# A build-time scheduler of a decoder trunk: transfers on one modelled rate, a reload in four lanes, a merge by accumulating transfers

## The chip, the cores and the metric

The kernel runs on one core of one Trainium2 chip. The metric is the device time of one execution in microseconds (us); the time before is the median of three runs. Engines are named as in the profile: PE (TensorE matmul), PEld (TensorE weight load), DVE (VectorE), ACT (ScalarE), POOL (GpSimd) and SP (SyncE, which here only issues transfers).

## The reference

One layer of a hybrid decoder trunk for a sequence of 512 tokens and 1024 channels in float32. Three token mixers stand side by side; their outputs go through one matrix each, are gated per channel, added, projected and added to the input.

```python
h = rmsnorm(x, norm_g)
proj = jnp.einsum('bsd,dn->bsn', h, w_in)
(aq, ak, av, ao, az, ai, af, bq, bk, bv, bz, bf, cu, cz, gates) = jnp.split(proj, SPLIT_POINTS, axis=-1)
...
yA = (hA.reshape(B, S, ML_WIDTH).astype(x.dtype) * ml_norm_g
      * jax.nn.sigmoid(ao) * jax.nn.silu(az))
...
yB = hB.reshape(B, S, FOX_WIDTH) * jax.nn.silu(bz)
...
ys = jnp.stack([yA, yB, yC], axis=2)
yb = jnp.einsum('bsnw,nwd->bsnd', ys, w_branch)
g = jax.nn.sigmoid(gates.reshape(B, S, N_BRANCH, D_MODEL))
merged = jnp.sum(g * yb, axis=2)
return x + jnp.einsum('bsd,de->bse', merged, w_out)
```

hA comes from a chunked mLSTM with 4 heads, hB from a forgetting attention with 8 heads, yC from a causal pooling with 4 groups. A last rmsnorm follows.

## The kernel before, in words

**Arithmetic.** Every float32 operand is split into a rounded part hi (a cast on ACT, line L291) and a remainder lo (a subtraction on DVE, L294); a product is three matmuls, hi·hi, hi·lo and lo·hi (`mm3`, L303 to L305). Activations stand channel by token: a weight tile of 128x128 is held in PE while 512 tokens (or 256) stream past.

**Weights.** They come from DRAM either as a unit (`feed_unit`: one transfer of 512 KB, L343 on SP, into a tile `raw`, then hi on ACT and lo on DVE) or as a pair (`feed_pair`). A pair serves two output chunks by seven products of half size in place of eight (a Strassen scheme). For it two transfers on SP (L379 of 512 KB, L383 of 768 KB) fill a tile `R`, and a third on POOL adds 512 KB to a part of it while it lands (L386, accumulating); two sums on DVE follow (L297). Out of R come four parts, numbered 0 to 3 in the trace of the order (hi_0, lo_0, ... hi_3, lo_3): part 1 comes straight from the L383 transfer, parts 2 and 3 need the sums. `raw` and `R` share three buffers. A pair's product writes three banks, named x, yz and y4 (the last prints as y); ACT copies a bank out (`side`, L497, L499; for the turned pairs of V L566) before PE may write the next product into it.

**Order of the work.** The four mixers' projections, heads and gates run first; then the three branches through their matrices, n = 0, 2, 1 in that order (wb in the trace), the merge, the output projection (out) and the last norm. The middle branch (n = 2, the pooling one) uses pairs whose moving operands ycs2, ycs3, ycs4 are sums made in `sides_c` (L1668 on); the last branch (n = 1, the attention) reads units. Branch outputs were written to DRAM (y) as they were made; `reload` (L1617) brings them back: eight transfers of 256 KB (`yf`, L1628) with a cast to hi and a lo each. Gates come back the same way (`gt`, L1752, 256 KB each).

**The scheduler.** Nothing is reordered on the chip: each engine runs its queue in the order in which the program emitted it, and a queue's head that waits holds all behind it. The order is fixed while the kernel is built, by the class `Flow`. Work beside the matmuls is written as chains, generators that yield (engine, cost, earliest start); `Flow` keeps a model clock for every engine, and emits the chain step that could start first, with a priority number to break ties. What a transfer takes is a constant in such a chain: a 512 KB raw unit lands 4.2 us after its issue whatever else is in flight, an R half 4.5 or 5.0, the accumulating part 6.2, a yf tile 6.0, and an issue on SP costs 0.06 us. So an instruction that waits for a transfer is put into its engine's queue where the model thinks that the transfer has landed.

**The merge of the middle branch** (L1789 to L1803): for each of four pairs, DVE multiplies two 128x512 halves of the result `ybc` by their gates (L1797), and then adds the whole 128x1024 tile to `mg` (the list `merged`), the running sum of the branches:

```python
                t = yield ("DVE", v_cost(D), t)
                add(merged[i], merged[i], c_)
                fl.put("C", 1, t)
```

The last branch adds to the same tiles: `gt<-wb,gt` (L1772), then `mg<-mg,gt` (L297), then the split into m for the output projection.

Of the kernel before, what the change touches and what calls it, by code (L numbers as in the profile page):

```python
# [10 lines left out]
ALU = mybir.AluOpType  # L11
# [3 lines left out]
S = 512  # L15
# [17 lines left out]
RAWS = 3  # L33

# [67 lines left out]
def a_cost(n):  # L102
    return 0.2 + 0.83e-3 * n
# [12 lines left out]
class Flow:  # L116
# [6 lines left out]
    def __init__(self):  # L123
        self.t = {"PE": 0.0, "DVE": 0.0, "ACT": 0.0, "POOL": 0.0, "SP": 0.0}
        self.func = None
        self.chains = []
        self.free = {}
        self.done = {}
        self.pos = 0

# [122 lines left out]
def trunk(tc, x, xt_in, w, wpair, cols, fg, out):  # L253
    nc = tc.nc
    with contextlib.ExitStack() as ctx:
# [75 lines left out]
        def feed_unit(i):  # L331
            what = order[i][1:]
            n = width(what)
            own = what[0] == "pw"
            prio = late(i, 0)

            def gen():
                if not own:
                    ts = yield ("get", "slot", 1)
                t = yield ("get", "R", 1)  # L340
                t = yield ("SP", 0.06, t)
                raw = raw_tile(f"raw{i}", n)
                nc.sync.dma_start(out=raw, in_=w[index[i]][:, :n])  # L343
                if own:
                    yield ("wait", ("av", AH - 1))
                    ts = yield ("get", "v", 1)
                t = max(t + 4.2, ts)
# [12 lines left out]
            fl.add(gen(), prio)  # L360

        def feed_pair(i, ps=None, q=None):
# [11 lines left out]
            def load():  # L374
                t = yield ("get", "R", 1)
                t = yield ("SP", 0.06, t)
                r = raw_tile(f"R{i}_{q}", 5 * Q)
                cell.append(r)
                nc.sync.dma_start(out=r[:, 3 * Q:].rearrange("p (a c) -> p a c", a=2),  # L379
                                  in_=src.rearrange("p (a c) -> p a c", c=Q)[:, 0:3:2])  # L380
                t1 = t + 4.5
                t = yield ("SP", 0.06, t)
# [538 lines left out]
        def emat(h):  # L921
# [4 lines left out]
            t = yield ("SP", 0.06, max(t, tw))  # L926
            nmb = work(f"nmb{h}")
            nc.sync.dma_start(out=nmb, in_=rows[h:h + 1, :].partition_broadcast(P))
            t = yield ("POOL", 0.9, t + 6.8)
# [105 lines left out]
        def values_a(h):  # L1035
# [68 lines left out]
            t = yield ("SP", 0.06, t)  # L1104
            nc.sync.dma_start(out=yd[0, h], in_=env["g"])
            fl.put("C", 1, t + 4.5)
            fl.done["y", 0, h] = t + 6.0
# [228 lines left out]
        def store(dst, tl, key, t):  # L1336
            def gen():
                t_ = yield ("SP", 0.06, t)
                nc.sync.dma_start(out=dst, in_=tl)
                fl.put("C", 1, t_ + 4.5)  # L1340
                fl.done[key] = t_ + 6.0
            fl.add(gen(), 0)
# [132 lines left out]
        def fox_pair(hp):  # L1475
            zB = [None]

            def head(h, cell, t_in):
# [14 lines left out]
                tn = yield ("SP", 0.2, tn)  # L1493
# [5 lines left out]
                tn += 8.0  # L1499
# [117 lines left out]
        def reload(n, homes, prio):  # L1617
# [4 lines left out]
            def one(i, c):  # L1622
# [19 lines left out]
            for i in range(4):  # L1642
                for c in range(2):
                    fl.add(one(i, c), prio)
# [32 lines left out]
        def sides_c():  # L1677
# [5 lines left out]
            for q in (2, 3, 0, 1):  # L1683
                for i in range(2):
                    ty = yield ("wait", ("y", 2, 2 * (q % 2) + i))
                    t = yield ("SP", 0.06, max(t, ty))
                    nc.sync.dma_start(out=f_[q][:, 2 * i:2 * i + 2],
                                      in_=yd[2, 2 * (q % 2) + i][:, :, (q // 2) * H:(q // 2 + 1) * H])
                tq.append(t + 9.0)
# [19 lines left out]
            t = max(tq)  # L1709
            yield from parts("A22", 3, home(0), t)  # L1710
# [35 lines left out]
        def load_gate(n, d):  # L1746
            def gen():
                tw = yield ("get", "w", 1)
                tg = yield ("wait", ("g", n, d // 2))
                t = yield ("SP", 0.06, max(tw, tg))  # L1750
                g_ = gate[n, d] = work(f"gt{n}{d}")
                nc.sync.dma_start(out=g_, in_=gd[n, d // 2][:, d % 2])  # L1752
                fl.done["gt", n, d] = t + 4.6
# [225 lines left out]
```

## Time and profile before

| | us |
|---|---|
| median of 3 runs | 856.97 (854.39, 856.97, 857.01) |
| profiled execution, whole time | 853.38 |
| its span | 851.4 |
| PE busy in the span | 835.8 (98%) |
| DVE busy | 663.1 (78%) |
| ACT busy | 535.4 (63%) |
| POOL busy | 114.0 (13%) |
| DMA, mean rate over the span | 187 GB/s, 158.96 MB |

The span is what the profiler saw of one execution; 2.0 us lie around it. A share is a share of the span. PE is one long stream of matmuls, so the rows to look for are those in which PE has a hole: in a timeline the idle time before an instruction stands in brackets, with the instruction whose end let it go.

### The profile page before, as it was taken

Reading aid. Unit: us, or ns where it says so; the run is one execution under the profiler, and the core shown is the slowest. Engines: PE = TensorE matmul, PEld = TensorE weight load, DVE = VectorE, ACT = ScalarE, POOL = GpSimd, SP = SyncE. Lnnn points to the kernel's source line nnn. Section 1 sums busy time; section 2 is a strip of 40 time slices with the busy share of each in tenths; the row PEclk is TensorE's granted clock in tenths of the full one; section 3 lists DMA queues with packets and bytes.
Section 4 is the critical chain, followed back from the end, with each engine's and each line's share of the span. In section 5 each row is a group of like instructions: output and inputs, shape, how many; then the busy total and the mean of one; then the engine's idle time right before and its main releaser. Section 6 shows DMA issues by size and latency. Waiting matters only on the chain.

```text
span 851.4 us, 15247 instructions
## 1 busy us (share of the span) xinstructions
PE 835.8 (98%) x6026; PEld 792.1 (93%) x6026; DVE 663.1 (78%) x1042; ACT 535.4 (63%) x906; POOL 114.0 (13%) x145
## 2 busy tenths in 40 slices
PE   9999999999999999999899999999999999999997
PEld 7888899999999999999899999999999988998886
DVE  5788998687998777988589788888887576986623
ACT  7569778757967857555367667568587553633223
POOL 0001422111111011010212111221220001010020
PEclk9999999999999999999999999999999999999999
DMA  9327866675774658487548878388865689576202
GB/s 342 110 75 221 215 172 173 194 203 117 214 191 112 186 159 215 136 251 195 153 161 219 225 179 241 91 208 246 239 143 199 206 280 321 157 275 219 102 22 99
DMA packets 62854, 158.96 MB, mean 187 GB/s; under 512 B 5428, under 2 KB 10932, under 8 KB 62784
## 3 DMA queue, kind: packets, MB, share of 16 engines
q1 hardware_dynamic: 47136, 126.96, 42.0%
q0 software_dynamic: 14928, 29.91, 20.9%
q10 hardware_dynamic: 720, 1.13, 0.4%
q8 instruction: 47, 0.77, 0.4%
q14 instruction: 23, 0.19, 0.1%
HBM read 143.27 MB, written 14.70 MB: 186 GB/s over the span
## 4 chain that ended last, share of the span: by engine, by line
PE 45%; DVE 2%; issue 1%; DMA 1%; ACT 1%; SPq 0%; DVEq 0%; ACTq 0%
PE wb L304 2%; PE wb L303 2%; PE wb L305 2%; PE out L304 2%; PE out L305 2%; PE out L303 2%; PE tpB L1562 1%; DMA yf<-y 1%; DVE lo L294 1%; DVE ycf L1703 1%; PE sB L304 0%; PE sB L303 0%; PE oB L303 0%; PE oB L304 0%; PE oB L305 0%
## 5 line engine op out<-in xcount | busy, mean ns | idle before, releaser
L294 DVE TENSOR_TENSOR lo<-R_None,hi 128x1024 fp32r<-128x1024 f32 (+1 forms) x184 | 197.8, 1091 | 30.2 <-ACT hi L291 29.7
L291 ACT CAST hi<-R_None 128x1024 fp32r<-128x1024 f32 (+1 forms) x184 | 169.1, 945 | 45.4 <-DVE R_None L297 26.0
L386 POOL DMA_DIRECT2D R_None<-w_pairs x46 | 56.0, 1217 | 461.4 <-DMA R_None<-w_pairs 211.5
L294 DVE TENSOR_TENSOR lo<-raw,hi 128x1024 fp32r<-128x1024 f32 (+3 forms) x45 | 51.5, 1151 | 25.7 <-ACT hi L291 25.4
L291 ACT CAST hi<-raw 128x1024 fp32r<-128x1024 f32 (+3 forms) x45 | 44.2, 994 | 40.9 <-DMA raw<-w_units 34.6
L297 DVE TENSOR_TENSOR R_None<-R_None 128x512 f32<-128x512 f32 x92 | 63.3, 689 | 2.5 <-DMA R_None<-w_pairs 1.7
L294 DVE TENSOR_TENSOR lo<-R,hi 128x1024 fp32r<-128x1024 f32 (+1 forms) x24 | 25.9, 1095 | 14.9 <-ACT hi L291 14.7
L291 ACT CAST hi<-R 128x1024 fp32r<-128x1024 f32 (+1 forms) x24 | 22.0, 942 | 8.7 <-DVE R L297 7.2
L304 PE MATMUL out<-lo,m 128*128 128x512 f32 (+1 forms) x72 | 26.3, 366 | 0.0
L303 PE MATMUL out<-hi,m 128*128 128x512 f32 (+1 forms) x72 | 26.3, 366 | 0.0
L305 PE MATMUL out<-hi,m 128*128 128x512 f32 (+1 forms) x72 | 26.3, 365 | 0.0
L1502 POOL TENSOR_SCALAR_AFFINE_SELECT nfb<-nfb 128x128 f32<-128x128 f32 x32 | 19.1, 731 | 31.1 <-DMA nfb<-rows 30.8
L1830 DVE TENSOR_TENSOR res<-out,res 128x512 f32<-128x512 f32 (+1 forms) x9 | 5.7, 632 | 18.4 <-PE out L305 18.2
L1833 ACT ACTIVATE fsq<-res 128x512 f32<-128x512 f32 (+1 forms) x9 | 5.3, 585 | 23.1 <-DVE res L1830 23.1
L291 ACT CAST m<-mg 128x512 fp32r<-128x512 f32 x8 | 5.0, 620 | 23.5 <-DVE mg L297 23.4
L1539 ACT ACTIVATE s<-s,mn 128x128 f32<-128x128 f32 (+3 forms) x32 | 17.8, 556 | 1.4 <-DVE mn L1528 1.3
L1528 DVE CUSTOM_DVE_ANT_0 s<-sB,nfb 128x128 f32<-128x128 f32 (+3 forms) x32 | 14.4, 485 | 4.0 <-issue 3.9
L303 PEld LDWEIGHTS out<-hi,m 128*128 128x128 f32 x72 | 13.6, 189 | 2.3
L304 PEld LDWEIGHTS out<-lo,m 128*128 128x128 f32 x72 | 13.6, 189 | 2.2
L305 PEld LDWEIGHTS out<-hi,m 128*128 128x128 f32 x72 | 13.6, 189 | 2.2
L386 POOL DMA_DIRECT2D R<-w_pairs x6 | 7.2, 1206 | 51.8 <-DMA R<-w_pairs 18.8
L1857 POOL TENSOR_TENSOR res<-res,fgb 128x512 f32<-128x512 f32 x4 | 5.2, 1296 | 65.3 <-ACT fsq L1833 65.1
(2495 smaller groups left out, 3533.2 us busy)
## 6 DMA issues: line engine op xcount, KB each, us to landing
R_None<-w_pairs SPq DMA_DIRECT2D x46, 768.0 KB, 6.9
R_None<-w_pairs SPq DMA_DIRECT2D x46, 512.0 KB, 4.8
R_None<-w_pairs POOLq DMA_DIRECT2D x46, 512.0 KB, 6.9
raw<-w_units SPq DMA_DIRECT2D x38, 512.0 KB, 4.5
g<-g SPq DMA_DIRECT2D x12, 512.0 KB, 5.4
gt<-g SPq DMA_DIRECT2D x24, 256.0 KB, 5.4
R<-w_pairs SPq DMA_DIRECT2D x6, 768.0 KB, 5.8
yf<-y SPq DMA_DIRECT2D x16, 256.0 KB, 6.3
```

Of the source, the lines that this page charges most:

```text
L291: nc.scalar.copy(out=hi, in_=full)
L294: nc.vector.tensor_tensor(out=lo, in0=full, in1=hi.bitcast(F32), op=ALU.subtract)
L297: nc.vector.tensor_tensor(out=out_, in0=a, in1=c, op=ALU.add)
L303: nc.tensor.matmul(out_, lhsT=ah, rhs=bh, start=start, stop=False, **kw)
L304: nc.tensor.matmul(out_, lhsT=ah, rhs=bl, start=False, stop=False, **kw)
L305: nc.tensor.matmul(out_, lhsT=al, rhs=bh, start=False, stop=stop, **kw)
L386: nc.gpsimd.dma_start(out=r[:, 3 * Q:].rearrange("p (a c) -> p a c", a=2), in_=src[:, 3 * Q:].unsqueeze(1).to_broadcast([P, 2, Q]), accum_ ...
L1502: nc.gpsimd.affine_select(out=nf[i][:, i * P:], in_=nf[i][:, i * P:], pattern=[[-1, P]], compare_op=ALU.is_ge, fill=NEG, base=0, channel_m ...
L1528: nc.vector.tensor_tensor_reduce(out=ss[i][:, :n], in0=os_[i][:, :n], in1=nf[i], scale=-P ** -0.5, scalar=-NEG, op0=ALU.add, op1=ALU.min, ...
L1539: nc.scalar.activation(out=s_, in_=s_, func=AF.Exp, bias=ms[i][0], scale=-1.0, accum_out=sme)
L1562: nc.tensor.transpose(tp[:, i * P:(i + 1) * P], ss[i][:, q0:q0 + P], ident)
L1703: nc.vector.tensor_tensor(out=f_[o], in0=f_[a_], in1=f_[c_], op=op)
```

## The change

It has four parts; what is computed stays the same, and so do all matmuls.

1. All modelled transfers share one rate. A new method `land` keeps the time at which the modelled bus comes free: a transfer lands 2.2 us after its issue or when the bus is free, whichever is later, plus its size over 260 KB per us (180 for accumulating ones, 100 and 150 for rows spread over the partitions). Every fixed landing is replaced by it, and an issue on SP costs 0.35 to 0.73 us in the model in place of 0.06 (2.9 for the four transfers of `nfb`), an accumulating issue on POOL 1.2 in place of 0.9.
2. The last branch is reloaded in four lanes of two tiles each, one after the other, at priority 1; before, eight chains stood side by side at priority 2.
3. The middle branch is merged by transfers: an accumulating transfer of 512 KB on POOL's queue from `ybc` to `mg` in place of the add on DVE, four times.
4. `sides_c` starts its A22 part when the second of four loads has landed in the model, not when all have.

```diff
+LATENCY = 2.2
...
+    def land(self, t, kb, rate=260.0):
+
+        self.bus = max(t + LATENCY, self.bus) + kb / rate
+        return self.bus
...
-                t = yield ("SP", 0.06, t)
+                t = yield ("SP", 0.55, t)
                 r = raw_tile(f"R{i}_{q}", 5 * Q)
...
-                t1 = t + 4.5
-                t = yield ("SP", 0.06, t)
+                t1 = fl.land(t, 512)
+                t = yield ("SP", 0.6, t)
                 nc.sync.dma_start(out=r[:, :3 * Q], in_=src[:, :3 * Q])
-                fl.done["R", me] = t + 5.0
-                t = yield ("POOL", 0.9, t1)
+                fl.done["R", me] = fl.land(t, 768)
+                t = yield ("POOL", 1.2, t1)
...
-                fl.done["T", me] = t + 6.2
+                fl.done["T", me] = fl.land(t, 512, 180.0)
...
-                tn = yield ("SP", 0.2, tn)
+                tn = yield ("SP", 2.9, tn)
...
-                tn += 8.0
+                tn = fl.land(tn - 2.0, 640, 150.0)
...
-        def reload(n, homes, prio):
+        def reload(n, homes, prio, lanes=8):
...
-                t = yield ("SP", 0.06, max(tw, ty))
+                t = yield ("SP", 0.73, max(tw, ty))
                 f_ = work(f"yf{n}{i}{c}")
                 nc.sync.dma_start(out=f_, in_=yd[n, i][:, c])
+                landed = fl.land(t, 256)
                 th = yield ("wait", ("home", n, i))
-                t = yield ("ACT", a_cost(S), max(t + 6.0, th))
+                t = yield ("ACT", a_cost(S), max(landed, th))
...
-            for i in range(4):
-                for c in range(2):
-                    fl.add(one(i, c), prio)
+
+            def lane(j):
+                for k in range(j, 8, lanes):
+                    yield from one(k // 2, k % 2)
+            for j in range(lanes):
+                fl.add(lane(j), prio)
...
-            t = max(tq)
-            yield from parts("A22", 3, home(0), t)
+            yield from parts("A22", 3, home(0), tq[1])
...
-        reload(1, home("yb"), 2)
+        reload(1, home("yb"), 1, 4)
...
-                t = yield ("DVE", v_cost(D), t)
-                add(merged[i], merged[i], c_)
-                fl.put("C", 1, t)
+                t = yield ("POOL", 1.2, t)
+                nc.gpsimd.dma_start(out=merged[i], in_=c_, accum_op=ALU.add)
+                fl.put("C", 1, fl.land(t, 512, 180.0))
```

Since the model decides the order, the numbers move instructions all over the program. Three places follow. In the rows an instruction stands with its line, its operation and its tiles; the number after a tile's name is a buffer's. Lines of the changed kernel lie 7 to 15 further down: L298 is the cast to hi, L301 lo, L304 the sum, L505 and L507 the copies of a bank, L574 that of a turned pair, L387, L391 and L394 the transfers of a pair, L1508 those of nfb, L1639 yf, L1767 gt, L1816 the new accumulating transfer.

**ACT, at the pair of bv in the attention heads** (`vbv_bv_1`, a turned pair whose weights stand in R_0 and R_1; hi_1 from R_None is a part of the next pair's weights). Before:

```order
L291 CAST dh_4607<-pb_4854 128x512
L291 CAST hi_1_5021<-R_None 128x512
L291 CAST hi_2_5024<-R_0_4656 128x1024
L566 COPY vbv_bv_1e_5041<-vbv_bv_1x 128x512
L291 CAST hi_2_5072<-R_1_4817 128x1024
L291 CAST hi_3_5082<-R_0_4656 128x1024
L291 CAST qkh_5105<-bqk_4989 128x1024
```

With the change:

```order
L298 CAST dh_4611<-pb_4837 128x512
L298 CAST hi_2_5042<-R_0_4667 128x1024
L298 CAST hi_2_5048<-R_1_4819 128x1024
L574 COPY vbv_bv_1e_5058<-vbv_bv_1x 128x512
L298 CAST hi_1_5089<-R_None 128x512
L298 CAST qkh_5085<-bqk_4991 128x1024
L298 CAST hi_3_5112<-R_0_4667 128x1024
L298 CAST hi_3_5134<-R_1_4819 128x1024
```

The cast hi_1 has moved behind both hi_2 and the copy of bank x; both hi_3 still stand behind it.

**ACT, at the first pair of the middle branch** (`wb_0_wb_1`; the four copies free its banks; yb0h, yb1h are casts of the last branch's reloaded tiles yf). Before:

```order
L497 COPY wb_0_wb_1e<-wb_0_wb_1x 128x256
L291 CAST yb0h<-yf_8732 128x512
L291 CAST hi_2_8794<-R_None 128x1024
L291 CAST yb0h<-yf_8734 128x512
L497 COPY wb_0_wb_1e<-wb_0_wb_1yz 128x256
L291 CAST yb1h<-yf_8736 128x512
L291 CAST yb1h<-yf_8738 128x512
L499 ACTIVATE wb_0_wb_1e<-wb_0_wb_1x 128x256
L291 CAST hi_3_8835<-R_None 128x1024
L497 COPY wb_0_wb_1e<-wb_0_wb_1y_8821 128x256
```

With the change:

```order
L505 COPY wb_0_wb_1e<-wb_0_wb_1x 128x256
L505 COPY wb_0_wb_1e<-wb_0_wb_1yz 128x256
L507 ACTIVATE wb_0_wb_1e<-wb_0_wb_1x 128x256
L505 COPY wb_0_wb_1e<-wb_0_wb_1y_8799 128x256
L298 CAST hi_2_8826<-R_None 128x1024
L298 CAST hi_1_8844<-R_None 128x512
L298 CAST hi_3_8848<-R_None 128x1024
L298 CAST hi_0_8871<-R_None 128x1024
L298 CAST yb0h<-yf_8743 128x512
```

No cast of a reloaded tile stands between the four copies any more; the first comes behind the four parts of the next pair.

**POOL, from the last attention head to the end of the middle branch.** Before:

```order
L1502 AFFINE_SELECT nfb_7485<-nfb_7485 128x128 x4
L1488 COPY qkf_7596<-bqk_7566 128x256
L386 DMA R_None<-w_pairs 128x2x512
L1502 AFFINE_SELECT nfb_7685<-nfb_7685 128x128 x4
L386 DMA R_None<-w_pairs 128x2x512 x5
L1813 DMA fgb<-final_g_in 128x1024
```

With the change:

```order
L1513 AFFINE_SELECT nfb_7683<-nfb_7683 128x128 x4
L394 DMA R_None<-w_pairs 128x2x512 x5
L1816 DMA mg_8442<-ybc_8830 128x1024
L1816 DMA mg_8519<-ybc_8957 128x1024
L1816 DMA mg_8602<-ybc_9093 128x1024
L1828 DMA fgb<-final_g_in 128x1024
```

Three of the new transfers stand between the last pair's accumulating transfer and the load of fgb; the fourth follows fgb and the four loads of res (x).

## Rows read from the trace of the kernel before

**Rows 1.** The page: busy time of each engine, share, instructions.

```profile
PE 835.8 (98%) x6026; PEld 792.1 (93%) x6026; DVE 663.1 (78%) x1042; ACT 535.4 (63%) x906; POOL 114.0 (13%) x145
```

**Rows 2.** What PE waited for: us in total, times, longest.

```profile
PE wb_wb_1yz L303 <- ACT wb_wb_1e L497: 2.3, 1, 2.3
PE vbv_bv_1z L303 <- ACT hi L291: 1.7, 1, 1.7
PE aq_aq_3y L305 <- DVE lo L294: 1.3, 1, 1.3
PE ak_ak_3yz L305 <- DVE lo L294: 0.8, 1, 0.8
```

**Rows 3.** PE's timeline at the bv pair: start, duration, instruction, [idle before].

```profile
422.70 0.40 PE L305 MATMUL py<-dh,lo 128*128 128x512 f32 x1
424.76 0.38 PE L303 MATMUL vbv_bv_1z<-hi,s1h 128*128 128x256 f32 x1 [1.67 <-ACT hi L291]
426.02 0.45 PE L304 MATMUL vbv_bv_1z<-lo,s1h 128*128 128x256 f32 x1 [0.88 <-DVE lo L294]
429.65 0.29 PE L303 MATMUL vbv_bv_1z<-hi,s1h 128*128 128x256 f32 x1
429.77 0.28 PE L304 MATMUL vbv_bv_1z<-lo,s1h 128*128 128x256 f32 x1
```

**Rows 4.** Windows there: busy us of PE, PEld, DVE, ACT, POOL; granted clock; DMA.

```profile
426.20:429.60 3.40, 3.14 (x14) 2.85 (x15) 3.38 (x6) 2.94 (x3) 0.00 (x0) 0.50 0.00 0
```

**Rows 5.** The timelines of SP's queue, DVE and ACT there.

```profile
410.12 2.87 SPq L1497 DMA_DIRECT2D nfb<-rows  x4
413.03 0.43 SPq L383 DMA_DIRECT2D R_None<-w_pairs  x1
...
414.11 0.68 DVE L297 TENSOR_TENSOR R<-R 128x512 f32<-128x512 f32 x1
...
423.14 0.62 ACT L291 CAST hi<-R_None 128x512 fp32r<-128x512 f32 x1 [8.90 <-DMA R_None<-w_pairs]
423.67 1.04 ACT L291 CAST hi<-R 128x1024 fp32r<-128x1024 f32 x1
```

**Rows 6.** PE's and ACT's timelines at the middle branch's first pair.

```profile
724.36 0.39 PE L303 MATMUL wb_wb_1yz<-ycs4h,hi 128*128 128x256 f32 x1 [2.32 <-ACT wb_wb_1e L497]
...
721.60 0.62 ACT L291 CAST yb0h<-yf 128x512 fp32r<-128x512 f32 x1 [4.85 <-DMA yf<-y]
723.94 0.37 ACT L497 COPY wb_wb_1e<-wb_wb_1yz 128x256 f32<-128x256 f32 x1
```

**Rows 7.** Windows by stage, columns as in rows 4.

```profile
50.00:100.00 50.00, 48.73 (x277) 42.75 (x276) 43.97 (x66) 44.02 (x57) 12.11 (x10) 1.00 0.61 180
725.00:750.00 25.00, 25.00 (x212) 25.00 (x211) 24.32 (x36) 15.31 (x27) 0.00 (x0) 1.00 0.48 154
```

**Rows 8.** Groups by line: busy us, mean ns, idle before.

```profile
L1122 ACT ACT_TABLE_LOAD x10 | 12.8, 1283 | 0.2
L297 DVE TENSOR_TENSOR mg<-mg,ybc 128x1024 f32<-128x1024 f32 x4 | 4.9, 1218 | 0.0
L386 POOL DMA_DIRECT2D R_None<-w_pairs x46 | 56.0, 1217 | 461.4 <-DMA R_None<-w_pairs 211.5
```

**Rows 9.** DVE's timeline at the end of the middle branch.

```profile
740.89 0.69 DVE L1797 TENSOR_TENSOR ybc<-ybc,gt 128x512 f32<-128x512 f32 x1
...
756.25 0.69 DVE L297 TENSOR_TENSOR ybc<-wb_wb_7yz,wb_wb_7e 128x512 f32<-128x512 f32 x1 [0.92 <-PE wb_wb_7yz L305]
756.85 1.22 DVE L294 TENSOR_TENSOR lo<-raw,hi 128x1024 fp32r<-128x1024 f32 x1
```

**Rows 10.** The page: transfers, KB each, median us from issue to landing.

```profile
R_None<-w_pairs SPq DMA_DIRECT2D x46, 512.0 KB, 4.8
R_None<-w_pairs POOLq DMA_DIRECT2D x46, 512.0 KB, 6.9
```

**Rows 11.** Line L386 from 72 to 76 us: issue to landing.

```profile
DMA to landing us min/median/max: 11.1/11.1/11.1
```

More of the change, by code (lines that the diff above doesn't have):

```diff
@@ L129, in __init__ @@
         self.pos = 0
+        self.bus = 0.0
+    def land(self, t, kb, rate=260.0):
+        self.bus = max(t + LATENCY, self.bus) + kb / rate
+        return self.bus
     def stock(self, name, n):
@@ L340, in gen @@
                 t = yield ("get", "R", 1)
-                t = yield ("SP", 0.06, t)
+                t = yield ("SP", 0.5, t)
                 raw = raw_tile(f"raw{i}", n)
                 nc.sync.dma_start(out=raw, in_=w[index[i]][:, :n])
+                landed = fl.land(t, n // 2)
                 if own:
@@ L346, in gen @@
                     ts = yield ("get", "v", 1)
-                t = max(t + 4.2, ts)
+                t = max(landed, ts)
                 t = yield ("ACT", a_cost(n), t)
@@ L380, in load @@
                                   in_=src.rearrange("p (a c) -> p a c", c=Q)[:, 0:3:2])
-                t1 = t + 4.5
-                t = yield ("SP", 0.06, t)
+                t1 = fl.land(t, 512)
+                t = yield ("SP", 0.6, t)
                 nc.sync.dma_start(out=r[:, :3 * Q], in_=src[:, :3 * Q])
-                fl.done["R", me] = t + 5.0
-                t = yield ("POOL", 0.9, t1)
+                fl.done["R", me] = fl.land(t, 768)
+                t = yield ("POOL", 1.2, t1)
                 nc.gpsimd.dma_start(out=r[:, 3 * Q:].rearrange("p (a c) -> p a c", a=2),
@@ L925, in emat @@
             tw = yield ("get", "w", 2)
-            t = yield ("SP", 0.06, max(t, tw))
+            t = yield ("SP", 0.7, max(t, tw))
             nmb = work(f"nmb{h}")
             nc.sync.dma_start(out=nmb, in_=rows[h:h + 1, :].partition_broadcast(P))
-            t = yield ("POOL", 0.9, t + 6.8)
+            landed = fl.land(t, 256, 100.0)
+            t = yield ("POOL", 0.9, landed)
             nmm = work(f"nmm{h}")
@@ L1103, in values_a @@
                 fl.put("mx", 1, t)
-            t = yield ("SP", 0.06, t)
+            t = yield ("SP", 0.35, t)
             nc.sync.dma_start(out=yd[0, h], in_=env["g"])
-            fl.put("C", 1, t + 4.5)
-            fl.done["y", 0, h] = t + 6.0
+            t = fl.land(t, 512)
+            fl.put("C", 1, t)
+            fl.done["y", 0, h] = t + 1.0
         def gate_a(h, z, o, t):
@@ L1337, in gen @@
             def gen():
-                t_ = yield ("SP", 0.06, t)
+                t_ = yield ("SP", 0.35, t)
                 nc.sync.dma_start(out=dst, in_=tl)
-                fl.put("C", 1, t_ + 4.5)
-                fl.done[key] = t_ + 6.0
+                t_ = fl.land(t_, 512)
+                fl.put("C", 1, t_)
+                fl.done[key] = t_ + 1.0
             fl.add(gen(), 0)
@@ L1685, in sides_c @@
                     ty = yield ("wait", ("y", 2, 2 * (q % 2) + i))
-                    t = yield ("SP", 0.06, max(t, ty))
+                    t = yield ("SP", 0.73, max(t, ty))
                     nc.sync.dma_start(out=f_[q][:, 2 * i:2 * i + 2],
                                       in_=yd[2, 2 * (q % 2) + i][:, :, (q // 2) * H:(q // 2 + 1) * H])
-                tq.append(t + 9.0)
+                    landed = fl.land(t, 256)
+                tq.append(landed)
             done = {}
@@ L1749, in gen @@
                 tg = yield ("wait", ("g", n, d // 2))
-                t = yield ("SP", 0.06, max(tw, tg))
+                t = yield ("SP", 0.4, max(tw, tg))
                 g_ = gate[n, d] = work(f"gt{n}{d}")
                 nc.sync.dma_start(out=g_, in_=gd[n, d // 2][:, d % 2])
-                fl.done["gt", n, d] = t + 4.6
+                fl.done["gt", n, d] = fl.land(t, 256)
             fl.add(gen(), 1)
```

## The prediction

> **What bounds the kernel now.** I began with the page's busy line: PE 98% of the span, DVE 78%, ACT 63% [rows 1]. PE bounds; and as the change leaves every matmul as it is, only the holes in PE's stream can be won. Of the 851.4 us of span PE is busy 835.8; the rest, 15.6 us, is the start, the tail after the last matmul and the holes. Next I read the list of what PE waited for: four waits of a size, 2.3, 1.7, 1.3 and 0.8 us [rows 2]. Each is for an instruction of ACT or DVE that is itself short; so the question at each is what stood ahead of it in its queue. The timelines answer that.
>
> *The bv pair.* PE ends py, begun at 422.70, waits 1.67 us for a hi, then 0.88 for its lo [rows 3]. In between and after, matmuls go at half pace: the window 426.2 to 429.6 has a granted clock of 0.50 [rows 4], the lower of the two levels, after PE had idled. ACT's timeline gives the cause: the cast hi from R_None stood idle 8.90 us for a transfer and began at 423.14, and the cast from R, which PE wanted, was behind it [rows 5]. The transfer was late since its SP issue (L383, at 413.03) came behind a 2.87 us issue of nfb [rows 5].
>
> *The first pair of the middle branch.* PE waits 2.32 us for the copy of a bank; on ACT that copy, 0.37 us long, starts at 723.94, behind casts of reloaded yf tiles, of which the first had waited 4.85 us for its transfer [rows 6].
>
> *The first heads.* DVE worked 43.97 us of 50 between 50 and 100 us [rows 7]; two lo come late, 1.3 and 0.8 us [rows 2].
>
> **The change, part by part.**
>
> *The shared rate, at bv.* ACT's queue as now emitted has both hi_2 and the copy of bank x ahead of hi_1. Both hi_2 need only sums, the later of which ran at 414.11 [rows 5], so they fit into the 8.90 us in which ACT idled. What goes with the wait: from 422.70 to 429.65 PE took 6.95 us; the work in it is one step of py (0.23) and 15 matmuls, which at the full clock follow each other by 0.12 (429.65 to 429.77 [rows 3]), 1.8 us. Lost: 6.95 - 0.23 - 1.80 = 4.9 us. I take all of it: -4.9. What is late next is hi_3, still behind hi_1: 423.14 + 0.5, then qkh and two more casts of about 1 us each [rows 5], so the second ends near 426.6, and its lo, 1.1 more, near 427.7. PE comes to them behind two products of 24 matmuls, 2.9 us each at 0.12, from 422.9 on: 428.7, and half a product later for the second. Cover of about 2 us. If the cover is gone, the hold is about 2 us and, with its half-clock stretch of up to 3.4 us [rows 4], gives back most of the 4.9: bounds -4.9 and -1.
>
> *The reload in lanes, at wb.* ACT's queue now has all four copies in a row, no cast of yf between; so the 2.32 us go, -2.3. The yf casts come after the next pair's four parts; the branch that reads them begins only after the middle branch, over 30 us on, so nothing waits for them soon. On SP, yf transfers now stand between the two halves of a pair's R; one issue costs about half a microsecond, and the half behind it lands that much later. In the last pair a hi_2 stands behind a yf cast; what that may cost is among the small waits below.
>
> *The shared rate, in the first heads.* DVE's order there puts another pair's lo_0 and a mixer's remainder behind the lo that PE waits for, and a scan ahead of it. Between nothing and both waits, 2.1 us [rows 2], I take -1.0: DVE stays too full there (88% [rows 7]) for all of it to go, since each thing put behind must still be done.
>
> *The merge by transfers.* Four adds of 1.218 us leave DVE [rows 8]: 4.9 us where it is 97% busy (24.32 of 25 [rows 7]), but PE is 25.00 of 25 in that window, so it counts nothing. Four issues of 1.217 us go to POOL [rows 8], idle at 87% [rows 1]. On POOL three of them stand ahead of fgb and res, needed only in the output projection; the fourth behind them, needed when the last branch adds to the last tile, some 30 us later. Their landing has no row, no transfer here adds SBUF to SBUF. Nearest rows: a plain transfer of the same size 4.8, the accumulating transfer 6.9 [rows 10], at the longest 11.1 [rows 11]. I take 6.9, since it too is an accumulating transfer of 512 KB from POOL. One instruction waits early: in the emitted order the result of the fourth pair (yz, on DVE) takes over the buffer that the first accumulating transfer reads. That transfer is issued after a product that ends at 741.6, and the result comes at 756.25 [rows 9]: 14.7 us for an issue of 1.2 and a landing of 6.9 to 11.1. It is covered; 0.
>
> [...]
>
> *ACT's function tables.* The emitted order has six more table loads on ACT, all in the first two fifths. A load is 1.283 us [rows 8]: 7.7 us of ACT, where it is busy 44.02 of 50 [rows 7]. That is hidden where ACT idles, and a wait of PE where a hi is due. Bounds 0 and +7.7; I take 0.5, since idle time is there and the order puts most loads next to the head's own work, not ahead of a due hi.
>
> The Trainium skill ("ScalarE: Activation LUTs", section "What ACT_TABLE_LOAD costs") gives 2.66 us for a switch with its drain; by it the upper bound would be 16 us. The trace's table loads stand idle 0.2 us in ten [rows 8], so no drain shows, and the measured time decides.
>
> *New small waits.* The order changes on nearly every queue, so some part of a weight will come later than before where it had little to spare. The smallest wait of a size here is 0.8 [rows 2]; one or two such: +1.0, bounds 0 and +4.
>
> **Sum**: -4.9 - 2.3 - 1.0 + 0.5 + 1.0 = -6.7 on the profiled execution's 853.4, so 846.7. That execution lies 3.6 under the median of the runs shown (856.97); the same shift gives **850.3** for the median, 0.8% faster. From here on 0.3%, about 2.6 us, is what a measurement can tell from no change.
>
> **Rivals.**
>
> *Half of it (0.15).* hi_3 at bv, or another cast of the shifted order, holds PE in turn, and the half-clock stretch comes back: of the 6.7 some 3 are left, 854. For it: the transfer is as late as before, since the SP rows at that place are the same. Against: a microsecond or two of cover.
>
> *No change (0.17).* The casts in the first 320 us come late behind six table loads: 7.7 us on ACT, most of which PE sees, since ACT is 88% busy there [rows 7]; 850.3 + 6 is 856. Or the model of transfers, though different, is no nearer to the real landings, and new holds as long as the old ones appear. For it: ACT and DVE have little room between 50 and 100 us. Against: PE's waits of a size for ACT were two, and neither lay there [rows 2].
>
> *Slower (0.12).* The accumulating transfers from SBUF to SBUF land late. The result of the fourth pair then holds DVE from 756.25 [rows 9], and behind it stand the lo of the last branch's units, the first at 756.85 [rows 9], which PE wants at once. It decides from a landing of 14.7 - 1.2 = 13.5 us; every microsecond more is one of PE, less what lo are already made. A landing of 25 us costs 11.5, giving 862; slower by over 2.6 us than 857 needs 13.5 + 6.7 + 2.6 = 22.8. Against: twice the longest accumulating landing seen, 11.1 [rows 11]. [...] In this chance I count such a hold elsewhere in the late branches.
>
> **How the numbers follow.** My forecast has 0.56, with a range of its own of 847.7 to 853: at its lower end both waits of the first heads go and nothing new comes (-4.9 - 2.3 - 2.1 = -9.3), at its upper end table loads and new waits take 2.7 us more than the 1.5 that I count. The range for 8 in 10 reaches down to 845, since the fastest run shown lies 2.6 under the median, and up to 858, through the half and the no-change cases; it leaves out the slower one. Faster by over 0.3%: 0.56 + 0.15, and 0.71; same 0.17; slower 0.12.
>
> **What would show it.** Right: in the changed profile no wait of PE at vbv_bv_1z and none at wb_wb_1yz, a granted clock of 1.00 through 420 to 430, PE's waits under about 4 us together. The accumulating transfers on mg land in 6 to 11 us, and no DVE wait names them. Wrong: a new wait of over 2 us on a hi in the first 320 us (table loads), a wait of vbv_bv_1 on hi_3 with a half-clock window behind it, or DVE idle at ybc for a transfer from mg.

## The result, and the profile after

The changed kernel takes **846.19 us** (median of 4 runs, 845.99 to 846.42); the kernel before, now with a fourth run, 856.99 (854.39 to 857.23). Ratio 0.9889, 95% interval 0.9865 to 0.9912: faster by 1.1%. The forecast was 850.3, in a range of 845 to 858. The profiled execution took 845.99 with a span of 843.9; the one before 853.38 with 851.4. So in the profiles 7.5 us went, in the medians 10.8. The two differences are told apart below.

The page of the changed kernel, the busy line that answers to [rows 1]:

```profile
PE 832.7 (99%) x6026; PEld 790.5 (94%) x6026; DVE 659.6 (78%) x1038; ACT 543.3 (64%) x912; POOL 122.0 (14%) x149
```

ACT has six instructions more (the table loads, 8 us), DVE four less, POOL four more. What PE waited for (us in total, times, longest), answering to [rows 2]:

```profile
PE aq_aq_3y L312 <- DVE lo L301: 1.2, 1, 1.2
PE warm_ps L680 <- POOL ones L673: 1.0, 1, 1.0
PE g_g_7y L312 <- DVE lo L301: 1.0, 1, 1.0
PE av L311 <- DVE lo L301: 0.8, 1, 0.8
PE bz_bz_5y L312 <- DVE lo L301: 0.3, 1, 0.3
...
PE ak_ak_3y L312 <- DVE lo L301: 0.3, 1, 0.3
```

Neither the bv pair nor the first wb pair is in the list. The wait for ak has shrunk from 0.8 to 0.3, the one for aq is still there, and one of 1.0 us at a gate pair (g_g_7y, at 221.7 us) is new. All waits together, small ones included, fell from 9.7 to 5.4 us.

Windows of PE's stretch at bv and of the middle branch (busy us of PE, PEld, DVE, ACT, POOL; granted clock; DMA share; GB/s), answering to [rows 4] and [rows 7]:

```profile
426.20:429.60 3.40, 3.40 (x28) 3.27 (x28) 2.76 (x11) 3.35 (x8) 0.00 (x0) 1.00 0.00 0
...
725.00:750.00 25.00, 25.00 (x212) 25.00 (x211) 21.47 (x32) 15.16 (x26) 2.31 (x3) 1.00 0.69 201
```

The granted clock is 1.00 where it was 0.50, with twice the matmuls in the same 3.4 us. In the middle branch DVE has 21.47 us of work in 25 in place of 24.32.

ACT's timeline of the changed kernel at both places (start, duration, instruction, [idle before]), answering to [rows 5] and [rows 6]:

```profile
415.02 2.01 ACT L298 CAST hi<-R 128x1024 fp32r<-128x1024 f32 x2 [3.42 <-issue]
416.93 0.57 ACT L574 COPY vbv_bv_1e<-vbv_bv_1x 128x512 f32<-128x512 f32 x1
418.44 0.62 ACT L298 CAST hi<-R_None 128x512 fp32r<-128x512 f32 x1 [0.94 <-DMA R_None<-w_pairs]
...
714.27 0.37 ACT L505 COPY wb_wb_1e<-wb_wb_1yz 128x256 f32<-128x256 f32 x1 [2.44 <-PE wb_wb_1yz L312]
715.72 0.39 ACT L507 ACTIVATE wb_wb_1e<-wb_wb_1x 128x256 f32<-128x256 f32 x1 [1.07 <-PE wb_wb_1x L312]
717.15 0.37 ACT L505 COPY wb_wb_1e<-wb_wb_1y 128x256 f32<-128x256 f32 x1 [1.05 <-PE wb_wb_1y L312]
717.42 3.46 ACT L298 CAST hi<-R_None 128x1024 fp32r<-128x1024 f32 x4
720.79 0.61 ACT L298 CAST yb0h<-yf 128x512 fp32r<-128x512 f32 x1
```

Now the copies wait for PE, not PE for the copies; the first yf cast comes when all four are through. At bv the cast from R_None idles 0.94 us where it idled 8.90: the casts from R ran first.

**Where the 7.5 us went.** The first matmul of a tile in both traces, read off the views of one tile: vbv_bv_1x starts at 414.4 before and 413.4 after; the next pair, bz_bz_1x, at 445.1 and 439.2; the first wb pair at 714.7 and 709.8; the last wb pair's wb_wb_7x at 747.4 and 739.9; the last matmul of all at 845.26 and 837.82. The lead over the kernel before is thus 1.0 us ahead of bv, 5.9 behind it (+4.9), 4.9 ahead of the middle branch (1.0 given back), 7.5 behind its first pair (+2.6), and 7.4 at the end. The matmuls are the same 6026, though some stand in another order; from each of these tiles to the next the same ones run in both kernels. Of the 7.4 us, 4.3 are shorter waits and 3.1 a shorter busy time (835.8 to 832.7), most of that at bv: PE is busy 28.1 us there before and 26.0 after for the same 201 matmuls, with the half-clock window in it.

The accumulating transfers to mg, in the changed kernel (POOL's timeline, then issue to landing of line L1816):

```profile
737.59 0.91 POOL L1816 DMA_DIRECT2D mg<-ybc  x1 [15.78 <-DVE ybc L1812]
747.39 0.86 POOL L1816 DMA_DIRECT2D mg<-ybc  x1 [8.90 <-DVE ybc L1812]
749.46 0.86 POOL L1816 DMA_DIRECT2D mg<-ybc  x1 [1.21 <-DVE ybc L1812]
...
753.75 0.88 POOL L1816 DMA_DIRECT2D mg<-ybc  x1 [0.75 <-DVE ybc L1812]
```

```profile
DMA to landing us min/median/max: 5.7/8.8/20.3
```

Taken one by one they land after 8.1, 5.7, 9.5 and 20.3 us. The fourth, behind fgb and four loads of res, is the long one. No instruction waited for any of them.

### The profile page after: what moved, and what is told of

It reads as the page before. It is cut to its first block, busy times and chain, and to the rows that moved or that the text cites. A ratio compares the mean times of both kernels' runs of the same rounds, so it can differ in the third digit from the quotient of the medians.

```text
span 843.9 us, 15268 instructions
## 1 busy us (share of the span) xinstructions
PE 832.7 (99%) x6026; PEld 790.5 (94%) x6026; DVE 659.6 (78%) x1038; ACT 543.3 (64%) x912; POOL 122.0 (14%) x149
## 4 chain that ended last, share of the span: by engine, by line
PE 87%; DVE 6%; ACT 3%; DMA 3%; issue 1%; SPq 0%; DVEq 0%; ACTq 0%
PE wb L311 4%; PE wb L310 3%; PE wb L312 3%; PE out L310 2%; PE out L311 2%; PE out L312 2%; DVE lo L301 2%; DMA R_None<-w_pairs 1%; PE tpB L1573 1%; PE av L311 1%; PE av L312 1%; PE av L310 1%; DMA x<-x_in 1%; PE num L1064 1%; PE num L1060 1%
## 5 line engine op out<-in xcount | busy, mean ns | idle before, releaser
L301 DVE TENSOR_TENSOR lo<-R_None,hi 128x1024 fp32r<-128x1024 f32 (+1 forms) x184 | 197.6, 1089 | 30.5 <-ACT hi L298 29.0
L298 ACT CAST hi<-R_None 128x1024 fp32r<-128x1024 f32 (+1 forms) x184 | 168.7, 944 | 33.9 <-DVE R_None L304 24.7
L394 POOL DMA_DIRECT2D R_None<-w_pairs x46 | 55.9, 1216 | 448.3 <-DMA R_None<-w_pairs 166.4
L304 DVE TENSOR_TENSOR R_None<-R_None 128x512 f32<-128x512 f32 x92 | 63.4, 689 | 7.2 <-DMA R_None<-w_pairs 6.2
L301 DVE TENSOR_TENSOR lo<-raw,hi 128x1024 fp32r<-128x1024 f32 (+3 forms) x45 | 51.5, 1153 | 14.0 <-ACT hi L298 14.0
L298 ACT CAST hi<-raw 128x1024 fp32r<-128x1024 f32 (+3 forms) x45 | 44.2, 994 | 16.1 <-DMA raw<-w_units 12.9
L301 DVE TENSOR_TENSOR lo<-R,hi 128x1024 fp32r<-128x1024 f32 (+1 forms) x24 | 25.9, 1091 | 3.7 <-ACT hi L298 3.4
L1513 POOL TENSOR_SCALAR_AFFINE_SELECT nfb<-nfb 128x128 f32<-128x128 f32 x32 | 21.6, 728 | 44.2 <-DMA nfb<-rows 35.4
L298 ACT CAST hi<-R 128x1024 fp32r<-128x1024 f32 (+1 forms) x24 | 22.5, 944 | 8.2 <-DVE R L304 3.7
L298 ACT CAST m<-mg 128x512 fp32r<-128x512 f32 x8 | 5.0, 621 | 30.6 <-DVE mg L304 30.6
L1785 DVE TENSOR_TENSOR mg<-wb,gt 128x512 f32<-128x512 f32 x8 | 5.5, 690 | 15.7 <-DMA gt<-g 15.7
```

The lines of the kernel that those rows point to most:

```text
L298: nc.scalar.copy(out=hi, in_=full)
L301: nc.vector.tensor_tensor(out=lo, in0=full, in1=hi.bitcast(F32), op=ALU.subtract)
L304: nc.vector.tensor_tensor(out=out_, in0=a, in1=c, op=ALU.add)
L1513: nc.gpsimd.affine_select(out=nf[i][:, i * P:], in_=nf[i][:, i * P:], pattern=[[-1, P]], compare_op=ALU.is_ge, fill=NEG, base=0, channel_m ...
```

## The experiments

Each run was compared with runs of the kernel before on the same chip; four kernels at a time. The first four ran beside a median of 855.24 for the kernel before (17 runs, 852.51 to 858.83), the second four beside 855.18 (851.28 to 857.05), the last four beside 854.90 (852.12 to 857.30). The three groups ran on three chips; a difference between runs of two groups has that in it too.

| run | median us | lowest to highest | ratio to before, 95% interval |
|---|---|---|---|
| e1, shared rate only | 850.16 | 848.59 to 850.51 | 0.9934 [0.9912, 0.9956] |
| e2, changed, no lanes | 848.99 | 848.70 to 849.44 | 0.9925 [0.9904, 0.9946] |
| e3, changed, no merge by transfers | 847.33 | 847.18 to 847.74 | 0.9906 [0.9883, 0.9929] |
| e4, before, with the merge alone | 854.72 | 852.52 to 858.50 | 0.9997 [0.9979, 1.0014] |
| e5, before, one landing at bv | 849.68 | 848.44 to 851.51 | 0.9935 [0.9915, 0.9955] |
| e6, before, landing of all yf | 854.96 | 853.49 to 856.96 | 1.0001 [0.9987, 1.0015] |
| e7, before, e5 and e6 | 849.47 | 849.40 to 851.04 | 0.9937 [0.9916, 0.9958] |
| e8, the changed kernel again | 846.29 | 845.93 to 846.51 | 0.9894 [0.9874, 0.9914] |
| e9, before, e5 and last branch's yf | 847.37 | 846.61 to 848.22 | 0.9916 [0.9899, 0.9933] |
| e10, changed, rate not shared | 852.85 | 851.55 to 853.75 | 0.9978 [0.9966, 0.9990] |
| e11, changed, rate 300 | 845.44 | 844.86 to 847.32 | 0.9897 [0.9879, 0.9915] |
| e12, changed, latency 3.0 | 846.44 | 845.77 to 847.77 | 0.9906 [0.9888, 0.9925] |

### Parts taken out, and one part alone

**e1, the shared rate alone.** From the changed kernel:

```diff
-        reload(1, home("yb"), 1, 4)
+        reload(1, home("yb"), 2)
...
-                t = yield ("POOL", 1.2, t)
-                nc.gpsimd.dma_start(out=merged[i], in_=c_, accum_op=ALU.add)
-                fl.put("C", 1, fl.land(t, 512, 180.0))
+                t = yield ("DVE", v_cost(D), t)
+                add(merged[i], merged[i], c_)
+                fl.put("C", 1, t)
```

> The changed kernel without the lanes (eight chains at priority 2 again) and without the accumulating merge (add on DVE again): the shared rate and the start of A22 alone. Theory 1, the shared rate carries the gain: the four copies of the first wb pair still stand in a row on ACT, so both big waits stay away; within 1.5 us of the changed kernel, 845 to 848, ratio near 0.989. Theory 2, the lanes take the 2.3 us wait at wb away (the step as I predicted it): the wait of wb_1yz is back, 848.5. Theory 3, DVE time freed by the merge matters late: four adds of 1.2 us back on DVE, up to 851.

850.16. None of the theories as I put them: both big waits stay away, without the lanes, yet some 4 us of the changed kernel's gain are missing. PE's list of waits shows two new ones:

```profile
PE wb_wb_7y L310 <- ACT hi L298: 1.4, 1, 1.4
PE wb_wb_7y L312 <- DVE lo L301: 0.8, 1, 0.8
```

Together they are 2.2 us. The rest is the clock behind them, 0.93 of full over these 20 us (columns as in the windows above):

```profile
750.00:770.00 20.00, 20.00 (x96) 17.19 (x96) 16.95 (x22) 6.68 (x8) 0.00 (x0) 0.93 0.83 297
```

(1.4 us of full-clock work lost here, a little more just ahead of it.) ACT's timeline has what made the first wait:

```profile
744.65 0.37 ACT L505 COPY wb_wb_7e<-wb_wb_7yz 128x256 f32<-128x256 f32 x1 [2.50 <-PE wb_wb_7yz L312]
744.92 1.05 ACT L298 CAST hi<-raw 128x1024 fp32r<-128x1024 f32 x1
746.09 0.38 ACT L507 ACTIVATE wb_wb_7e<-wb_wb_7x 128x256 f32<-128x256 f32 x1
746.37 1.04 ACT L298 CAST hi<-R_None 128x1024 fp32r<-128x1024 f32 x1
```

In the last pair the cast that PE needs stands behind a copy that itself waited 2.50 us for PE, and behind a cast of raw: the same kind of hold as before, at another pair. In the changed kernel that cast runs at 741.83, ahead of the copy. So the shared rate alone closes both holes that the prediction named, and opens one in the last pair.

**e2, without the lanes.**

```diff
-        reload(1, home("yb"), 1, 4)
+        reload(1, home("yb"), 2)
```

> The changed kernel with the last branch reloaded by eight chains at priority 2 as before. Theory 1: 846, nothing comes back, since the order of the copies at the first wb pair is the same. Theory 2: 848.5 with a wait of about 2.3 us at wb_1yz.

848.99, the size that theory 2 gave and not for its reason: at wb_1yz there is no wait. Two others have come in the last branch, as PE's waits show:

```profile
PE wb L312 <- DVE lo L301: 2.2, 2, 1.1
```

SP's own longest wait for a gate between 735 and 765 us, and what stands ahead of the first of PE's two waits, on DVE and on ACT:

```profile
SPq L1767 <- DVE yb0l L301: 9.5, 1, 9.5
```

```profile
764.99 0.69 DVE L1787 TENSOR_TENSOR gt<-wb,gt 128x512 f32<-128x512 f32 x1 [3.15 <-DMA gt<-g]
...
767.70 1.22 DVE L301 TENSOR_TENSOR lo<-raw,hi 128x1024 fp32r<-128x1024 f32 x1
```

```profile
766.44 0.62 ACT L298 CAST m<-mg 128x512 fp32r<-128x512 f32 x1 [4.93 <-DVE mg L304]
766.97 1.04 ACT L298 CAST hi<-raw 128x1024 fp32r<-128x1024 f32 x1
```

The lo that PE waits for until 769.0 is a remainder of `raw`; its hi stands on ACT behind a cast of `mg`, and that behind a product with a gate on DVE, which waited 3.15 us for the gate's transfer. The first two such products of the last branch start at 757.91 and 764.99, in the changed kernel at 756.29 and 763.16. With eight yf tiles asked for at once, a gate's load on SP stood 9.5 us until the first of them, yb0l, was done with and its buffer free; gates and raw units alternate behind it in SP's queue, and the first raw unit is issued at 739.32, in the changed kernel at 737.94, where the gates' loads wait 2.3 us in all in that stretch. That the late gates begin with this hold is read off SP's queue; no run has it alone. So the lanes are worth 2.7 us (848.99 less 846.29, on two chips), but in the last branch, not at wb.

**e3, without the merge by transfers.** The second piece of e1's diff alone.

> The changed kernel with the middle branch merged by an add on DVE. Theory 1: 846, as PE has no hole where the adds stand; DVE's busy time up by 4.9 us. Theory 3: slower by 1 to 5 us, with a wait of PE for a lo of the last branch.

847.33, 1.0 us more than the changed kernel (846.29 in e8), and no runs of the two overlap, though they ran on two chips. In the traces the stretch from wb_wb_7x to the output projection is longer by 1.3 us (55.5 against 54.2). Theory 3 in its mildest form: one wait more,

```profile
PE wb_wb_7yz L312 <- DVE lo L301: 0.8, 1, 0.8
```

for a lo of the middle branch's last pair, not of the last branch: one add of 1.22 us stands ahead of it in DVE's queue at 738.83.

**e4, the merge alone on the kernel before.**

```diff
-                t = yield ("DVE", v_cost(D), t)
-                add(merged[i], merged[i], c_)
+                t = yield ("POOL", 0.9, t)
+                nc.gpsimd.dma_start(out=merged[i], in_=c_, accum_op=ALU.add)
-                fl.put("C", 1, t)
+                fl.put("C", 1, t + 6.2)
```

> The kernel before with the accumulating merge alone. Theory 1: same as before within 0.3%, 854 to 858; both big waits stay (4.9 us around bv, 2.3 at wb). Theory 3: faster by 1 to 5 us. The rival of the late landing: landings over 13 us, DVE waiting on the buffer of ybc, slower.

854.72 against 855.24, as theory 1 had it: no difference, though the interval leaves room for a microsecond either way. The traces are sharper: from wb_wb_7x to the output projection PE takes 54.1 us with the merge and 54.1 without. So the merge gives its microsecond (e3) only where the other holds are gone. The new transfers landed after 4.7 to 13.5 us, and nothing on DVE waited for one.

This trace shows something else. Up to the bv pair every queue is that of the kernel before, and the same hole is there, 3.1 us of waits; but no stretch at half clock follows it. It follows the wait at wb. Windows of the kernel before, then two of e4:

```profile
420.00:430.00 10.00, 7.20 (x38) 6.05 (x37) 5.24 (x7) 4.99 (x6) 0.94 (x3) 0.83 0.34 84
```

```profile
420.00:430.00 10.00, 6.87 (x46) 5.65 (x45) 6.54 (x8) 4.99 (x6) 0.64 (x2) 1.00 0.29 61
...
700.00:725.00 25.00, 22.32 (x127) 19.68 (x126) 16.85 (x21) 9.97 (x15) 3.62 (x3) 0.97 1.00 304
```

So the same hole is followed by half clock in one execution and not in another. From vbv_bv_1x to bz_bz_1x PE takes 30.7 us in the trace of before, 30.0 in this one, and 25.8 without the hole (e5 and the changed kernel).

### The two holes one by one

**e5, one landing at bv.** Item 46 of the weights' order is that pair.

```diff
-                fl.done["R", me] = t + 5.0
+                fl.done["R", me] = t + (10.0 if i == 46 else 5.0)
```

> The kernel before with one number changed: the second half of the one pair whose SP issue stands behind the four nfb transfers at bv lands 10.0 us after its issue in the model, not 5.0. SP's queue is unchanged; ACT has both hi_2, the copy of bank x and one hi_3 ahead of hi_1. Theory 1 (the hole at bv comes from that one cast's place): PE's waits at vbv_bv_1z go, 4.9 us less in the profile; and as the spread of the kernel before (852.5 to 858.8) went with its granted clock, 0.991 to 0.998, the half-clock stretches behind this hole go too: median 849 to 851, spread under 2 us. Rival: the next cast in the row (hi_3 of R_1, behind hi_1 still) holds PE in its place, and less than 2 us is gained.

849.68: 5.5 us from one constant. SP's queue is unchanged and the transfer lands as late as ever, at 423.66; ACT merely has something else to do until then:

```profile
418.35 2.00 ACT L291 CAST hi<-R 128x1024 fp32r<-128x1024 f32 x2
423.66 0.62 ACT L291 CAST hi<-R_None 128x512 fp32r<-128x512 f32 x1 [3.30 <-DMA R_None<-w_pairs]
```

and PE waits for nothing at bv. The rival (hi_3 takes its place) falls: one hi_3 moved ahead too. Between the two tiles around bv the trace gains 4.9 us, as in the changed kernel. The spread is 3.1 us, not under 2: the profiled execution is the longest of the six, and has a half-clock stretch at the other hole, behind a wait of 3.6 us at wb_1yz.

```profile
700.00:725.00 25.00, 21.41 (x125) 19.37 (x124) 16.62 (x22) 9.69 (x16) 3.64 (x3) 0.93 1.03 305
```

**e6, the landing of every yf tile.**

```diff
-                t = yield ("ACT", a_cost(S), max(t + 6.0, th))
+                t = yield ("ACT", a_cost(S), max(t + 12.0, th))
```

> The kernel before with one number changed: a reloaded yf tile lands 12 us after its issue in the model, not 6. Eight chains as before. The four copies of the first wb pair then have no cast of yf between them. Theory 1: the wait at wb_1yz goes, 2.3 to 2.7 us; the hole at bv and the spread stay: median 852 to 853.5. Rival (as at the run with the shared rate alone, where 2.2 us of waits came at wb_7y): the yf casts now hold a later pair, and nothing is gained.

854.96, no gain. The wait at wb_1yz is gone, but the same constant served the first reload as well, and moved its casts (ya2h, ya3h) into a gate pair that was free of them. First PE's waits, then ACT's timeline at that pair:

```profile
PE g_g_7yz L303 <- ACT g_g_7e L497: 1.4, 1, 1.4
PE g_g_7x L303 <- ACT g_g_7e L499: 1.0, 1, 1.0
```

```profile
667.81 1.04 ACT L291 CAST hi<-raw 128x1024 fp32r<-128x1024 f32 x1 [2.43 <-DMA raw<-w_units]
668.76 0.37 ACT L497 COPY g_g_7e<-g_g_7yz 128x256 f32<-128x256 f32 x1
```

**e7, both.** e5's and e6's lines together.

> The kernel before with both numbers. Theory 1: the two holes account for nearly all of the gain: 846 to 849, at most 2 us above the changed kernel. Rival, the shared rate as a whole does more than those two places: 850 or above.

849.47: between theory and rival by its number, and the waits say why: the 2.3 us at the gate pair are those of e6.

**e8, the changed kernel again.**

> The changed kernel again, on the same chip as the three others: 845.5 to 846.5 with a spread under 1 us.

846.29, as expected.

**e9, both holes, and only those.**

```diff
-                fl.done["R", me] = t + 5.0
+                fl.done["R", me] = t + (10.0 if i == 46 else 5.0)
...
-                t = yield ("ACT", a_cost(S), max(t + 6.0, th))
+                t = yield ("ACT", a_cost(S), max(t + (12.0 if n == 1 else 6.0), th))
```

> The kernel before with two numbers changed at two places: the late half at bv lands after 10 us in the model, and yf tiles of the last branch alone land after 12 (the first reload keeps 6, so the gate pair where the run with both landings lost 2.3 us has its old order). Theory 1, the two holes are most of the gain: 846.5 to 848.5, spread under 2 us. Rival: the casts put off at wb hold the fourth pair of the middle branch, as with the shared rate alone: 849 or more.

847.37: by the ratios two numbers give 0.84% of the 1.06% that the whole change gave in e8. PE has no wait at bv and none at the first wb pair. A part of the rival is true as well; PE waits 1.2 us in the last pair:

```profile
PE wb_wb_7y L305 <- DVE lo L294: 0.8, 1, 0.8
...
PE wb_wb_7y L303 <- ACT hi L291: 0.4, 1, 0.4
```

### Is it the sharing?

**e10, later landings that do not share a rate.**

```diff
-        self.bus = max(t + LATENCY, self.bus) + kb / rate
-        return self.bus
+        return t + 4.2 + kb / rate
```

> The changed kernel with landings that do not share a rate: a transfer lands 4.2 us plus its size over 260 KB per us after its issue, whatever else is in flight (6.2 for 512 KB, 7.2 for 768 KB, near the medians of the profile). All else as changed. In the emitted order hi_1 stands ahead of the copy of bank x at bv again, and one yf cast ahead of the copy at wb. If the sharing is what counts, both holes come back at least in part: 850 to 856, and a spread of several us. If it is only that landings are told later, 846 to 848.

852.85: most of the gain is gone, but only one of the two holes is back. At bv PE does not wait (the transfer had landed by 417.35). At the first wb pair it waits more than ever; PE's waits, then ACT's timeline:

```profile
PE wb_wb_1x L309 <- ACT wb_wb_1e L506: 5.4, 1, 5.4
```

```profile
714.90 0.37 ACT L504 COPY wb_wb_1e<-wb_wb_1yz 128x256 f32<-128x256 f32 x1
720.81 0.62 ACT L297 CAST yb0h<-yf 128x512 fp32r<-128x512 f32 x1 [5.55 <-DMA yf<-y]
```

The model believed that a yf tile lands 5.2 us after its issue (4.2 plus 256 over 260), with a pair's two SP transfers, 1.25 MB, issued just ahead of it; the cast stood 5.55 us, and the copy that PE needed next stood behind it. The four tiles issued together there landed after 9.8 to 10.1 us.

So these constants leave a hole that the shared rate doesn't. It is not shown that every set of constants would: 5.2 us for a yf tile is less than the 6.0 of the kernel before, where such a tile took 6.3 at the median, and e9, with 12 us for the last branch's tiles and no sharing, has no wait at this pair.

**e11 and e12, other numbers in the shared model.** `rate=300.0` in place of 260, and `LATENCY = 3.0` in place of 2.2.

> The changed kernel with a shared rate of 300 in place of 260. Both places keep their order. If the two holes are what counts: 845 to 848.5, other small waits taking the place of those in the changed kernel. If the exact rate matters: off by more than 2.6 us.

> The changed kernel with a latency of 3.0 in place of 2.2. Both places keep an order without the holds. Same forecast as for the rate: 845 to 848.5; it would beat the changed kernel only if the waits of 1.2 us (aq) and 1.0 us (a gate pair) go without others in their place.

845.44 and 846.44. Neither can be told from the changed kernel, though nearly every queue has another order. e11 has the lowest median of all, 0.8 us under e8, but its runs reach from 844.86 to 847.32, so it isn't shown to beat it. In e12 a wait of 1.9 us for a lo of the last branch has taken the place of those at aq and at the gate pair.

## Why the prediction was right, and where not

**The hole at bv, -4.9: right.** Between the same two tiles the changed kernel gains 4.9 us, and so does e5, from that place alone (5.5 in its median). The cover that I named for hi_3, about 2 us, held. The transfer was late by more than the 2.87 us issue ahead of it: issued at 413.03, it took 10.1 us to land, where the model had 5.0. One thing I took as unchanged was not: the SP rows at that place are in the same order, but they ran 4 us earlier (the L391 issue at 409.09, not 413.03), so the transfer landed at 418.44. e5, where it lands at 423.66, shows that the order alone would have done. And a part of the 4.9 is the half-clock stretch, which the sum took as sure: in the trace it begins at 426.2, not "in between" the two waits, and in e4 the hole costs 4.2 us without one.

**The hole at wb, -2.3: right in size, wrong in its cause.** The lead grows by 2.6 us there. But the step "The reload in lanes, at wb" gave it to the lanes, and e1 and e2 have no wait there without them, with every queue the changed kernel's up to 716 us; the shared rate put the copies in a row. In e2 the lanes turn out to be worth 2.7 us in the last branch, where I had said that nothing waits soon: the eight tiles hold buffers that the gates' loads on SP need, the gates come later, and two lo that PE wants stand behind products with them.

**The merge, 0: mis-sized by 1.0 us.** "PE is 25.00 of 25 in that window, so it counts nothing" read a window in which the hole stood elsewhere. Once the bv and wb holes are gone, an add puts off a lo of the last pair (e3: 0.8 us of wait). Alone, on the kernel before, the merge does count nothing (e4). Its landing, taken as 6.9 with 11.1 as the longest, was 5.7 to 9.5 for three and 20.3 for the fourth, beyond my bound; it was needed only at 789.5, 36 us after its issue, and no one waited.

**The first heads, -1.0, and new waits, +1.0: right in sum, not in their causes.** The lead before bv is 1.0 us, but PE's waits up to there did not shrink: 4.6 us before, 4.9 after. The wait at aq lost 0.1 and the one at ak 0.5; the new 1.0 at the gate pair took that back. It is PE's busy time for the same matmuls that fell, by 1.3 us, and part of that is the execution: with the kernel before's queues up to that point, vbv_bv_1x starts at 413.6 in e4 and at 414.7 in e5, against 414.4 in the profiled execution. The five traces with the changed order there (the changed kernel's two, e1, e2, e3) have 413.3 to 413.6, so something of it is the order's; but not by the waits named, and the size came out by luck. The other 1.0, given back between bv and the middle branch, is 0.5 us of small waits (bq_bk_4yz 0.2, bz_bz_5y 0.3) and 0.5 of a longer busy time; what made that longer, no run shows. The prediction's list of "four waits of a size" also left out two lines of that view: 1.1 us for the lo at bv, of which it gives 0.88 elsewhere, and 0.8 at av, which is still there (0.8).

**Table loads, +0.5.** ACT's six more loads show in its busy time (543.3 against 535.4), and PE has no wait over 0.3 us for ACT. One load in the changed kernel, with its neighbours:

```profile
426.06 0.62 ACT L298 CAST hi<-R 128x512 fp32r<-128x512 f32 x1
426.70 1.28 ACT L1550 ACT_TABLE_LOAD   x1
428.00 0.40 ACT L1550 ACTIVATE s<-s,mn 128x128 f32<-128x128 f32 x1
```

The cast ends at 426.68, the load takes 1.28, and the next instruction starts at 428.00: the drain that the Trainium skill ("ScalarE: Activation LUTs", section "What ACT_TABLE_LOAD costs") adds, 2.66 us together, is not there. The new accumulating issues cost POOL 0.86 to 0.91 us each, less than the 1.217 that the prediction took; three of them fall in the 25 us in which DVE is busy 21.47.

**The sum and the median.** On the profiled execution the sum said 846.7, and it was 845.99. That it fits so well is in part luck. The shared rate alone closes both holes but brings 3.9 us back in the last pair (e1, 850.16 against 846.29), where the sum had +1.0 for new waits; the lanes (2.7) and the merge (1.0), for which the sum had the wrong place and nothing, keep those out, and the errors nearly cancel. The miss of 4 us in the median, 850.3 against 846.19, is the step that put the prediction 3.6 us above the profiled execution, as the median of before lay: "the same shift".

That shift belonged to the kernel before, and it goes with the clock. Its 51 runs beside the experiments reach from 851.28 to 858.83. Those with a mean granted clock of 0.999 (2 runs) take 851.4 us in the mean, with 0.997 (24 runs) 854.0, with 0.993 (10 runs) 856.6. A clock lower by 0.006 over 853 us is 5.1 us of full-clock work, and the means lie 5.1 apart. The changed kernel's nine runs, 845.93 to 846.51, all have 0.998 or 0.999. Start and end apart, every half-clock stretch in the profiles of this case stands in or behind a hole: at bv (before, e6), at wb (e4, e5, e10) or in the last pair (e1). So the longer executions are those with more time at half clock; that it lies behind the two holes in them too is an inference, since no long execution of the kernel before was profiled. The spreads fit it only roughly: 6.0 and 3.5 us where the hole at bv is kept (e4, e6, 12 runs each), 2.2 where only one at wb is (e10, 12 runs), 3.1, 1.6 and 1.6 for the kernel before without the hole at bv (e5, e7, e9, 6 runs each).

**The rivals.** "Half of it" and "slower" did not come; no instruction waited for a transfer to mg. "No change" had one true element that I had put in the wrong place: holds do move when the order is shuffled (e1, e2, e6, e12), but to the late branches; in the first 320 us the changed kernel has one new wait of 1.0 us. Of the signs that were named, the two big waits gone and a clock of 1.00 came; PE's waits came to 5.4 us together (1.0 of it at the start of the kernel), not under 4, and one of the four transfers to mg landed far later than 11.

## What to carry to other kernels

On in-order queues a short cast that waits for a transfer costs little itself; the price is what stands behind it. A hole in the matmul stream costs its length and, in some executions, a stretch at half clock after it (2.8 us of waits at bv, 4.9 lost with such a stretch, 4.2 without in e4). Where a program decides the order at build time, a model in which transfers share one rate found both places without being told of them, and its exact rate mattered little (e11, e12). The one set of constants tried in its place left a hole (852.9 in e10, against 846.2); two constants set by hand where a trace had shown the holes came within about a microsecond of it (847.4 in e9). Cost a part of a change with the other parts in place: the merge, worth nothing that could be measured on the kernel before, gave 1.0 us once the larger holes were closed.

## What was not expected

An accumulating transfer of 512 KB from SBUF to SBUF lands in 5.7 to 9.5 us, about as one from DRAM (7.4 median in the changed kernel), but in 20.3 behind 2.5 MB of loads on the same queue. And one constant, a landing of 10 us in place of 5 for one transfer among hundreds, was worth 5.5 us (e5), some six tenths of what the whole change gave beside it (8.9 in e8). It is about what that transfer takes (10.1 us in the trace of before).
